# Issuing the middle result store from GpSimd instead of SyncE, in a row-wise ReLU-sum kernel

## The chip, the core and the metric

The kernel runs on one core of one Trainium2 chip. The metric is device time in microseconds for one execution of the whole program; for the kernel before, three runs were made and their median is given. A profile is one further execution, taken by the hardware profiler. It covers the span from the first to the last instruction that belongs to the kernel; the time of the execution is somewhat longer than the span.

## What is computed

```python
def setup_inputs():
    batch, seq, dim = 32, 512, 1024
    return {"x": np.random.randn(batch, seq, dim).astype(np.float32)}

def reference(x):
    relu_x = np.maximum(x, 0)
    return np.sum(relu_x, axis=-1).astype(np.float32)
```

There are 32 x 512 = 16384 rows of 1024 floats. Each row gives one float: the sum of its positive elements. 67.1 MB are read, 65.5 KB are written.

## The kernel before

**Layout.** The 16384 rows are spread over 128 partitions, so each partition handles J = 128 rows, called columns 0 to 127 here, as each ends up in one column of the result tile `res` (128 x 128 floats). The columns are cut into three regions, `REGIONS = [1, 111, 16]`. Within a region a partition's rows lie next to each other in memory, so a load of n columns is one contiguous run of n x 4 KB per partition, and a store of n columns is one run of n x 4 bytes per partition: 4 bytes for the first region, 444 for the middle one, 64 for the last.

**Loads.** All loads are issued by SyncE, in the order of the code, each with its own semaphore `s_in[...]` (a DMA raises its semaphore by 16 when it has landed). Seven chunks of 16 columns (`CHUNKS`; the first one in two DMAs, as it holds the one column of the first region and 15 of the middle one) go to three buffers in turn. From the fourth chunk on, SyncE first waits on `s_dve` until VectorE is done with that buffer. Then come tail loads of 8, 4 and 2 columns (line 103), and the last two columns in four pieces: three on line 114 (the last of these is counted by `s_in[-1]`) and one on line 117 that crosses from one row into the next, into the tile `seam`.

**Arithmetic.** For the first six chunks ScalarE applies ReLU in place to several columns at a time (line 147) and VectorE sums them (line 162), apart from some columns that either engine does alone. In the seventh chunk and the tail, and for the columns done alone, one instruction does both: `on_act` (line 129) on ScalarE, `on_dve` (line 132) on VectorE, each followed by a read of the accumulator. In the seventh chunk (lines 175 to 181) the two engines take alternate columns; the last column of each raises `s_fdve` and `s_fact`, and columns 1 to 111 of `res` are complete when both have passed. The pieces of the last two columns put partial sums into `seam`, and one closing instruction on each of ScalarE and VectorE (lines 205 and 207) adds them up and raises `s_last`.

**Stores.** There are three, all issued by SyncE behind the loads:

- Line 119, the first region: column 0 is transposed by VectorE into the tile `turned` (line 171), so that the 128 results leave as 4 runs of 128 bytes. It waits on `s_turn` and raises `s_store`.
- Line 125, the middle region: columns 1 to 111, 128 runs of 444 bytes, 55.5 KB. It waits on `s_fact`, `s_fdve` and `s_in[-1]`; the last of these is the landing of a load, not of a result that the store needs. It raises `s_store`, too.
- Line 211, the last region: columns 112 to 127, 128 runs of 64 bytes, 8 KB. It waits on `s_last` and raises `s_out`.

SyncE then waits until `s_store` has 32 and `s_out` has 16 (lines 212 and 213), and the program ends. SyncE's instructions run in order, so a wait holds up everything that is written behind it on SyncE. GpSimd has no work in the kernel; it only fills four constants at the start.

Of the kernel before, what the change touches and what calls it, by code (L numbers as in the profile page):

```python
# [7 lines left out]
REGIONS = [1, 111, 16]  # L8
# [10 lines left out]
def bass_relu_sum_kernel(  # L19
# [26 lines left out]
    start = [sum(REGIONS[:i]) for i in range(len(REGIONS))]  # L46
# [4 lines left out]
    ov = [of[P * s : P * (s + n)].rearrange("(p j) -> p j", p=P) for s, n in zip(start, REGIONS)]  # L51
# [4 lines left out]
    res = nc.alloc_sbuf_tensor("res", [P, J], fp32)  # L56
# [3 lines left out]
    s_in = [nc.alloc_semaphore(f"s_in{i}") for i in range(n_in)]  # L60
    s_act = nc.alloc_semaphore("s_act")
    s_dve = nc.alloc_semaphore("s_dve")
    s_fact = nc.alloc_semaphore("s_fact")
    s_fdve = nc.alloc_semaphore("s_fdve")
# [2 lines left out]
    s_last = nc.alloc_semaphore("s_last")  # L67
    s_turn = nc.alloc_semaphore("s_turn")
    s_store = nc.alloc_semaphore("s_store")
    s_out = nc.alloc_semaphore("s_out")  # L70

    sp, act, dve = nc.sync, nc.scalar, nc.vector

    NTWO = len(ACT_STEPS)
    done = [sum(map(len, DVE_STEPS[: c + 1])) for c in range(NTWO)]
# [11 lines left out]
    for c in range(NBIG + 1):  # L87
        if c >= NB:
            sp.wait_ge(s_dve, done[c - NB])
        if c < NBIG:  # L90
            i = 0
            for g, j, n in CHUNKS[c]:
                sp.dma_start(  # L93
                    out=buf[:, c % NB, i : i + n, :], in_=xv[g][:, j : j + n, :]
# [18 lines left out]
    for k, (lo, hi) in enumerate((first, second, third)):  # L113
# [5 lines left out]
    sp.dma_start(  # L119
        out=of[0:P].rearrange("(k q) -> k q", q=32), in_=turned[0:P:32, 0:32]  # L120
    ).then_inc(s_store, 16)
    sp.wait_ge(s_fact, 1)
    sp.wait_ge(s_fdve, 1)
    sp.wait_ge(s_in[-1], 16)
    sp.dma_start(out=ov[1][:, :], in_=res[:, start[1] : start[2]]).then_inc(s_store, 16)


    def on_act(t, acc):
# [11 lines left out]
    for c in range(NTWO):  # L140
# [17 lines left out]
        for n in DVE_STEPS[c]:  # L158
            if ready[r + n - 1] > seen:
# [3 lines left out]
                out=res[:, c * BIG + r : c * BIG + r + n],  # L163
                in_=buf[:, c % NB, r : r + n, :],
# [44 lines left out]

    sp.wait_ge(s_last, 2)  # L210
    sp.dma_start(out=ov[-1][:, :], in_=res[:, start[-1] : J]).then_inc(s_out, 16)
    sp.wait_ge(s_store, 16 * (len(REGIONS) - 1))
    sp.wait_ge(s_out, 16)


# [26 lines left out]
```

## Time and profile before

| What | Value |
|---|---|
| median of 3 runs | 160.79 us (160.7 to 160.81) |
| the profiled execution, its time | 160.84 us |
| its span | 159.5 us |
| VectorE busy | 120.7 us (76%), 59 instructions |
| ScalarE busy | 101.5 us (64%), 54 instructions |
| GpSimd busy | 0.2 us, 4 instructions |
| read from memory, mean | 67.11 MB, 421 GB/s over the span |
| granted clock | 1.00 |

The profile's engines are PE (TensorE, unused here), DVE (VectorE), ACT (ScalarE), POOL (GpSimd) and SP (SyncE). A name with a q at its end, such as SPq, is that engine's instruction queue: waits, and the issuing of DMAs, which do not count as busy. `L125` is line 125 of the kernel. In the timeline a row has its start in us, its length in us, engine, line, operation, and the tiles written and read. A view by windows gives, for each stretch of the span, the busy time of each engine, the granted clock, the mean busy share of the 16 DMA engines, and the GB/s that they moved. The time from a DMA's issue to its landing is printed for those whose landing some instruction waited for last.

### The profile page before, as it was taken

The page shows a single profiled execution, that of the slowest core. Times are in us where ns is not written, and L with a number is a line of the kernel's source. Part 1 is how long each engine was busy: PE and PEld are TensorE (multiplying, and loading weights), DVE is VectorE, ACT ScalarE, POOL GpSimd, SP SyncE. Part 2 cuts the span into 40 slices and gives each one's busy share as a digit, 9 for nine tenths or more (in the row PEclk, how much of TensorE's full clock was granted, in tenths as well). Part 3 has the DMA queues.
Part 4 walks back from the last instruction along what each step waited for, and adds up shares of the span by engine and source line. Part 5 has one row for each costly group of instructions (what it writes and reads, how often), then busy time and mean ns, then how long its engine had stood idle before and what let it go on. Part 6 is the DMA issues. An engine that isn't in the chain of part 4 may idle for free.

```text
span 159.5 us, 150 instructions
## 1 busy us (share of the span) xinstructions
DVE 120.7 (76%) x59; ACT 101.5 (64%) x54; POOL 0.2 (0%) x4
## 2 busy tenths in 40 slices
DVE  0000000009999999999999999999999999898995
ACT  3000059990799708996099951999329990496975
POOL 0000000000000000000000000000000000000000
DMA  9997996996996998989969969969969989798994
GB/s 378 493 401 339 493 526 263 526 526 263 526 510 279 526 427 362 526 362 427 526 263 526 526 263 526 526 263 526 493 296 526 427 362 526 312 469 378 419 403 142
DMA packets 2457, 67.18 MB, mean 421 GB/s; under 512 B 536, under 2 KB 792, under 8 KB 1176
## 3 DMA queue, kind: packets, MB, share of 16 engines
q1 hardware_dynamic: 2456, 67.18, 98.1%
q14 instruction: 1, 0.01, 0.0%
HBM read 67.11 MB, written 0.07 MB: 421 GB/s over the span
## 4 chain that ended last, share of the span: by engine, by line
DVE 54%; DMA 34%; ACT 9%; SPq 1%; issue 0%
DVE res L162 54%; DMA buf<-in_x_dram 34%; ACT buf L147 9%; SPq L103 1%; SPq L114 0%; DVE seam L132 0%; SPq L93 0%; ACT buf L129 0%; DVE turned L171 0%
## 5 line engine op out<-in xcount | busy, mean ns | idle before, releaser
L162 DVE TENSOR_REDUCE res<-buf 128x4 f32<-128x4096 f32 (+4 forms) x16 | 99.3, 6275 | 35.6 <-ACT buf L147 35.6
L147 ACT ACTIVATE buf<-buf 128x7168 f32<-128x7168 f32 (+5 forms) x13 | 80.4, 6233 | 46.2 <-DMA buf<-in_x_dram 46.2
L129 ACT ACTIVATE buf<-buf 128x1024 f32<-128x1024 f32 (+2 forms) x19 | 18.9, 994 | 9.0 <-DMA buf<-in_x_dram 8.9
L132 DVE TENSOR_SCALAR_CACHE_REDUCE buf<-buf 128x1024 f32<-128x1024 f32 (+3 forms) x20 | 20.9, 1099 | 1.7 <-DMA buf<-in_x_dram 1.5
L129 ACT ACTIVATION_READ_ACCUMULATOR buf<-buf 128x1 f32 x19 | 3.5, 186 | 0.0
L147 ACT ACT_TABLE_LOAD x1 | 1.3, 1283 | 1.3 <-PEq L227 1.3
L132 DVE DVE_READ_ACCUMULATOR buf<-buf 128x1 f32 x20 | 1.7, 83 | 0.0
L132 DVE TENSOR_SCALAR_CACHE_REDUCE seam<-seam 128x227 f32<-128x227 f32 x1 | 0.4, 391 | 0.0
L129 ACT ACTIVATE seam<-seam 128x114 f32<-128x114 f32 x1 | 0.3, 298 | 0.0
L171 DVE STREAM_TRANSPOSE turned<-res 128x32 f32<-128x32 f32 x1 | 0.2, 211 | 0.0
L129 ACT ACTIVATION_READ_ACCUMULATOR seam<-seam 128x1 f32 x1 | 0.2, 186 | 0.0
L227 POOL MEMSET const-bfloat16-1.0<- 128x1 bf16 x1 | 0.1, 102 | 0.0
L227 POOL MEMSET const-uint8-127<- 128x1 uint8 x1 | 0.1, 102 | 0.0
L227 POOL MEMSET const-float32-0.0<- 128x1 f32 x1 | 0.1, 99 | 0.2 <-issue 0.2
L227 POOL MEMSET const-float32-1.0<- 128x1 f32 x1 | 0.1, 99 | 0.0
L132 DVE DVE_READ_ACCUMULATOR seam<-seam 128x1 f32 x1 | 0.1, 81 | 0.0
## 6 DMA issues: line engine op xcount, KB each, us to landing
buf<-in_x_dram SPq DMA_DIRECT2D x1, 7680.0 KB, 21.2
buf<-in_x_dram SPq DMA_DIRECT2D x1, 4096.0 KB, 25.5
buf<-in_x_dram SPq DMA_DIRECT2D x1, 2048.0 KB, 30.1
buf<-in_x_dram SPq DMA_DIRECT2D x1, 1024.0 KB, 32.1
buf<-in_x_dram SPq DMA_DIRECT2D x1, 512.0 KB, 3.4
buf<-in_x_dram SPq DMA_DIRECT2D x1, 456.0 KB, 32.7
buf<-in_x_dram SPq DMA_DIRECT2D x1, 312.0 KB, 33.1
seam<-in_x_dram SPq DMA_DIRECT2D x1, 168.0 KB, 32.7
```

The lines of the kernel that those rows point to most:

```text
L103: sp.dma_start(out=buf[:, tb, r : r + n, :], in_=xv[-1][:, r : r + n, :]).then_inc(s_in[NBIG + i], 16)
L129: return act.activation(t, t, AF.Relu, accum_out=acc)
L132: return dve.tensor_scalar(out=t, in0=t, scalar1=0.0, scalar2=None, op0=ALU.max, op1=ALU.add, accum_out=acc)
L147: act.activation(t, t, AF.Relu).then_inc(s_act, 1)
L162: dve.tensor_reduce(out=res[:, c * BIG + r : c * BIG + r + n], in_=buf[:, c % NB, r : r + n, :], axis=X, op=ALU.add,).then_inc(s_dve, 1)
L171: dve.transpose(out=turned[:, :], in_=res[:, 0:32]).then_inc(s_turn, 1)
L227: nc = _bacc.Bacc("TRN2", target_bir_lowering=False, num_devices=1)
```

## The change

The middle store and its three waits go to GpSimd's queue. The store gets a semaphore of its own, `s_bulk`. The transposed store alone raises `s_store` now, so SyncE's closing waits are three: `s_store` at 16, `s_bulk` at 16, `s_out` at 16. Loads, the transposed store and the last store stay on SyncE. One line is added near the top, so the middle store's issue is on line 126 and the last store's on line 212 afterwards.

```diff
+    s_bulk = nc.alloc_semaphore("s_bulk")
     s_out = nc.alloc_semaphore("s_out")
 
-    sp, act, dve = nc.sync, nc.scalar, nc.vector
+    sp, act, dve, pool = nc.sync, nc.scalar, nc.vector, nc.gpsimd
...
-    sp.wait_ge(s_fact, 1)
-    sp.wait_ge(s_fdve, 1)
-    sp.wait_ge(s_in[-1], 16)
-    sp.dma_start(out=ov[1][:, :], in_=res[:, start[1] : start[2]]).then_inc(s_store, 16)
+    pool.wait_ge(s_fact, 1)
+    pool.wait_ge(s_fdve, 1)
+    pool.wait_ge(s_in[-1], 16)
+    pool.dma_start(out=ov[1][:, :], in_=res[:, start[1] : start[2]]).then_inc(s_bulk, 16)
...
     sp.wait_ge(s_last, 2)
     sp.dma_start(out=ov[-1][:, :], in_=res[:, start[-1] : J]).then_inc(s_out, 16)
-    sp.wait_ge(s_store, 16 * (len(REGIONS) - 1))
+    sp.wait_ge(s_store, 16)
+    sp.wait_ge(s_bulk, 16)
     sp.wait_ge(s_out, 16)
```

## The prediction

> **What bounds the kernel now.** I read the page's chain of work first. It is a chain of the reductions and then of the loads, and it goes through no store until the very end:
>
> ```profile
> ## 4 chain that ended last, share of the span: by engine, by line
> DVE 54%; DMA 34%; ACT 9%; SPq 1%; issue 0%
> ```
>
> The store that is moved is issued at 157.22 us of a span of 159.5 us, so only the last 2.3 us are in question. The view of SyncE's queue waits says what SyncE stood at in that time (columns: who waited, for what, us in total, times, longest):
>
> ```profile
> SPq L124 <- DMA buf<-in_x_dram: 31.2, 1, 31.2
> ...
> SPq L213 <- DMA out_dram<-res: 1.1, 1, 1.1
> SPq L211 <- DVE seam L132: 0.4, 1, 0.4
> ```
>
> The reader is to see three things. The middle store (line 125) waits 31.2 us for the last load, s_in[-1], and nothing else holds it. After it, SyncE waits another 0.4 us for VectorE before the last store (line 211): SyncE was not late, VectorE was. And the end is the last store's landing. The timeline, cut to the last 3 us, gives the moments (start, duration, engine, line):
>
> ```profile
> 157.22 0.35 SPq L125 DMA_DIRECT2D out_dram<-res  x1
> ...
> 157.58 0.39 DVE L132 TENSOR_SCALAR_CACHE_REDUCE seam<-seam 128x227 f32<-128x227 f32 x1
> 157.78 0.19 ACT L129 ACTIVATION_READ_ACCUMULATOR seam<-seam 128x1 f32 x1
> 157.90 0.08 DVE L132 DVE_READ_ACCUMULATOR seam<-seam 128x1 f32 x1
> 158.00 0.34 SPq L211 DMA_DIRECT2D out_dram<-res  x1
> ```
>
> SyncE has finished issuing the middle store at 157.22 + 0.35 = 157.57, and VectorE's last instruction ends at 157.98; the last store starts 0.02 later. So SyncE has 0.43 us to spare, and taking the middle store off its queue cannot bring the last store forward. Where the two transfers' packets run is seen when the same stretch is cut into seven windows (window, length, DVE, ACT and POOL busy, granted clock, DMA share, GB/s):
>
> ```profile
> 157.20:157.57 0.37, 0.34 (x4) 0.35 (x2) 0.00 (x0) 1.00 0.00 0
> 157.57:158.08 0.51, 0.40 (x2) 0.39 (x2) 0.00 (x0) 1.00 0.00 0
> 158.08:158.43 0.35, 0.00 (x0) 0.00 (x0) 0.00 (x0) 1.00 0.57 163
> 158.43:158.84 0.41, 0.00 (x0) 0.00 (x0) 0.00 (x0) 1.00 0.00 0
> 158.84:159.06 0.22, 0.00 (x0) 0.00 (x0) 0.00 (x0) 1.00 0.42 38
> 159.06:159.32 0.26, 0.00 (x0) 0.00 (x0) 0.00 (x0) 1.00 0.00 0
> ```
>
> The 55.5 KB of the middle store move from 158.08 to 158.43: 0.86 us after the issue began, for 0.35 us (163 GB/s x 0.35 us = 57 KB, so it is this store). The 8 KB of the last store move from 158.84 to 159.06, also 0.84 us after its issue. The wait at line 213 ends at 159.44 (158.00 + 0.34 + the 1.1 us waited), which is 0.38 us after the last packet; its instruction then closes the span at 159.47. The middle store's landing is not printed. With the same 0.38 us after its last packet it is there at 158.43 + 0.38 = 158.81, which is 1.59 us after its issue and **0.63 us before the end**. That slack decides this change.
>
> **The change, part by part.**
>
> Removed from SyncE: three waits and one DMA issue of 0.35 us, at a place where SyncE then stands idle for 0.4 us. Gain: 0. The loads and the transposed store stand ahead of it on SyncE's queue and were issued by 125.9 us; they don't move. Behind it stand only line 211 and the closing waits. SyncE will wait for s_last from 125.9 us on instead of for the last load; the release at 157.98 is VectorE's in either case, so line 211 stays at 158.00.
>
> Added to GpSimd: the same three waits. GpSimd's only work is four MEMSETs before 0.5 us, so nothing is queued behind these waits and the wait itself is free: s_fact and s_fdve fall by 147.1 us (the last rows of the seventh chunk end there), s_in[-1] by 157.2, as for SyncE today. Then one DMA issue with 128 rows of 444 bytes. **Its price is the unknown**, since no row of this trace shows a DMA issued by GpSimd. Of the 1.59 us from issue to landing, 0.73 (packets 0.35, landing 0.38) belong to the data and stay; the 0.86 us of preparation are what another issuer changes.
>
> Low bound: GpSimd prepares as fast as SyncE, or faster. At 0.86 us the store lands at 158.81; at the least, were the issue's own 0.35 us gone, at 158.46. Neither moves the end, because the last store then sets it: 0. Nothing earlier can be gained than that.
>
> High bound: the longest landing of a transfer that started on an idle queue is the first load, 512 KB in 3.4 us, nine times the bytes, with others beside it:
>
> ```profile
> buf<-in_x_dram SPq DMA_DIRECT2D x1, 512.0 KB, 3.4
> ...
> out_dram<-res SPq DMA_DIRECT2D x1, 8.0 KB, 1.4
> ```
>
> With 3.4 us the store lands at 157.22 + 3.40 = 160.62. I take the middle of 1.59 and 3.4, which is 2.50 us: bytes and packets are those of the low row, so the preparation alone can grow, and 2.50 us means 1.77 us for it, twice the 0.86 shown. I lean no nearer to the low row because every landing in this trace was prepared by SyncE, so no row speaks for GpSimd being as quick; and no nearer to the high row because nine times the bytes are in it. Landing then: 157.22 + 2.50 = 159.72. Its packets would run at about 158.99 to 159.34, beside the last store's (158.84 to 159.06); the most that these can take from it is their own busy time, 0.42 x 0.22 = 0.09 us. Landing 159.81.
>
> The closing waits: the one instruction of 28 ns at line 213 holds both semaphores today (the view of that line counts one); three semaphores ask for one more, 0.03 us each, all of them behind the landing where the middle store is last. End: 159.81 + 0.03 + 0.03 = 159.87.
>
> **Sum:** 159.87 - 159.47 = **+0.40 us**. The profiled execution took 160.84 us for its 159.47 us of span, so 1.37 us lie around it, taken as unchanged: 161.24. The median of the runs is 160.79, 0.05 below that execution, so **161.2 us** (+0.25%). A difference of 0.2%, 0.32 us, is about what a measurement of this kernel can tell from no change.
>
> A rule against the change: the Trainium skill, "DMA: Bandwidth & Descriptors", section "Issuing engines are not separate DMA queues", says that DMAs of all issuers share the same 16 engines and that spreading them saves only issue time; the windows agree in so far as 0.35 us of issue is all that SyncE loses to it here, and none of it counts. The same page's section "Latency and other measured facts" has the first byte at about 1 us for GpSimd's software path and 0.6 us for the hardware path, and "Anatomy of one DMA" fits 2.0 us + bytes/436e3 per DMA issued by GpSimd. By that fit the landing would be an estimated 157.22 + 2.13 = 159.35, just inside the slack, and the time unchanged. No run here shows it, and the sum above stands without it.
>
> **Rivals.**
>
> 1. *Hidden: no change.* GpSimd's landing takes under 2.2 us (it must be in by 159.44). For it: the slack of 0.63 us is real and three quarters of today's preparation. Against it: preparation has to stay under 0.86 + 0.63 = 1.49 us. Time: 160.79, or 160.82 with one more closing wait.
>
> 2. *Faster: the last store gains.* Place: line 211. Its issue at 158.00 falls while the middle store is still on the same path (packets until 158.43), and its own packets come at 158.84, 0.50 after its issue ended. If a part of this 0.50 were the middle store ahead of it, a queue of its own would give it back: at most all of it, so 160.3. It decides only while the middle store lands before the new end, that is by 158.95 (issue to landing 1.73). Against it: the middle store, on a queue that had issued nothing for 31 us, had the same gap (157.57 to 158.08, 0.51). An empty path gives no less, so the gain is nearer 0.
>
> 3. *First use.* GpSimd has done nothing for 157 us, and this is its only DMA; if a first use has to load something, as ScalarE does at its start (ACT_TABLE_LOAD, 1.28 us), that comes on top of the sum: 161.2 + 1.28 = 162.5. Nothing in the trace speaks for it on GpSimd.
>
> That the change fails to do what it says (SyncE still issues the store) is out: the issue is written on the other queue, and the trace will name it.
>
> **How the numbers follow.** The forecast, the middle store lands last at +0.05 to +1.3 us (the high bound: 160.62 + 0.09 + 0.06 = 160.77, or +1.30): 0.62. Hidden: 0.25. Faster by the last store: 0.06. First use: 0.07. Within the forecast's own 0.05 to 1.3 some four fifths lie above 0.32 us: slower 0.50 + 0.07 = 0.57; same 0.12 + 0.25 = 0.37; faster 0.06. The point is the likeliest case's, 161.2. The range takes in the hidden case and all but the last tenth of the forecast's: 160.7 to 162.0.
>
> **What would show it.** A POOL row of line 126 at 157.2 with nothing ahead of it; the last store still at 158.00; the 163 GB/s window no longer at 158.08 but behind 158.5; the closing waits ending on the middle store's semaphore instead of the last store's. If the packets of the two stores overlap, the last store's landing shifts by up to 0.1 us. I am wrong if packets of 444 bytes run before 158.7 (hidden), if line 211 issues at another time than 158.00, or if the stretch outside the span is not 1.37 us.

## The result, and the profile after

Over 15 runs each, taken together, the kernel after the change has a median of **161.11 us** (160.98 to 161.26) against 160.79 us (160.66 to 160.95) for the kernel before: a ratio of 1.0021, 95% interval [1.0014, 1.0028]. It is 0.32 us slower. The profiled execution took 161.10 us with a span of 159.8 us (159.75 by its last instruction), so 1.35 us lie around the span, against 1.37 before: the loss is inside it.

The timeline of the kernel after, cut to the last 2.7 us (start, length, engine, line, idle time before it and what ended that):

```profile
157.12 0.33 DVE L133 TENSOR_SCALAR_CACHE_REDUCE buf<-buf 128x176 f32<-128x176 f32 x1
...
157.49 0.39 DVE L133 TENSOR_SCALAR_CACHE_REDUCE seam<-seam 128x227 f32<-128x227 f32 x1
157.68 0.66 POOL L126 DMA_DIRECT2D out_dram<-res  x1 [157.24 <-DMA buf<-in_x_dram]
157.70 0.19 ACT L130 ACTIVATION_READ_ACCUMULATOR seam<-seam 128x1 f32 x1
157.81 0.08 DVE L133 DVE_READ_ACCUMULATOR seam<-seam 128x1 f32 x1
157.92 0.35 SPq L212 DMA_DIRECT2D out_dram<-res  x1
```

VectorE's last piece starts at 157.49, and at 157.58 before: in this execution the loads landed 0.09 us earlier, which has to be kept in mind when moments of the two are compared. The last store starts 0.03 us after VectorE's last instruction, so it gained nothing. The middle store's row on GpSimd starts at 157.68, although the load that it waits for has landed by 157.1 (VectorE starts on that piece at 157.12, the first row shown). Before the change VectorE started on the same piece at 157.20, and SyncE's row began only 0.02 us later, at 157.22:

```profile
157.20 0.33 DVE L132 TENSOR_SCALAR_CACHE_REDUCE buf<-buf 128x176 f32<-128x176 f32 x1
```

And GpSimd's row is 0.66 us long against SyncE's 0.35.

The DMA view has the issue to landing of both stores; before, it was 1.4 for the last one:

```profile
out_dram<-res POOLq DMA_DIRECT2D x1, 55.5 KB, 2.0
...
out_dram<-res SPq DMA_DIRECT2D x1, 8.0 KB, 1.4
```

SyncE's waits say which store ended last:

```profile
SPq L212 <- DVE seam L133: 32.1, 1, 32.1
...
SPq L214 <- DMA out_dram<-res: 1.4, 1, 1.4
```

Line 214 is the wait on `s_bulk`. It holds from 157.92 + 0.35 = 158.27 until about 159.67; line 215, `s_out`, waits for nothing any more, so the middle store now ends the program. Where the packets ran (window, length, DVE, ACT, POOL, clock, DMA share, GB/s):

```profile
157.68:158.34 0.66, 0.21 (x2) 0.20 (x2) 0.66 (x1) 1.00 0.00 0
158.34:158.76 0.42, 0.00 (x0) 0.00 (x0) 0.00 (x0) 1.00 0.00 0
158.76:158.92 0.16, 0.00 (x0) 0.00 (x0) 0.00 (x0) 1.00 0.52 48
158.92:159.26 0.34, 0.00 (x0) 0.00 (x0) 0.00 (x0) 1.00 0.56 169
159.26:159.75 0.49, 0.00 (x0) 0.00 (x0) 0.00 (x0) 1.00 0.00 0
```

The order of the two stores has turned round: the last store's 8 KB move from 158.76 and are all but over when the middle store's 55.5 KB begin at 158.92. From the start of its row to its packets GpSimd's store takes 1.24 us; SyncE's took 0.86. The packets themselves take as long as before (0.34 and 0.35 us).

### The profile page after: what moved, and what is told of

The parts are those of the page before. It is cut to its first block, busy times and chain, and to the rows that moved or that the text cites. A ratio compares the mean times of both kernels' runs of the same rounds, so it can differ in the third digit from the quotient of the medians.

```text
span 159.8 us, 151 instructions
## 1 busy us (share of the span) xinstructions
DVE 120.7 (76%) x59; ACT 101.5 (64%) x54; POOL 0.9 (1%) x5
## 4 chain that ended last, share of the span: by engine, by line
DVE 54%; DMA 34%; ACT 9%; SPq 2%; issue 1%; POOL 0%; POOLq 0%
DVE res L163 54%; DMA buf<-in_x_dram 34%; ACT buf L148 9%; SPq L104 1%; SPq L115 1%; POOL out_dram L126 0%; SPq L94 0%; DVE turned L172 0%; POOLq L125 0%
## 5 line engine op out<-in xcount | busy, mean ns | idle before, releaser
L126 POOL DMA_DIRECT2D out_dram<-res x1 | 0.7, 662 | 157.2 <-DMA buf<-in_x_dram 157.2
```

The source lines that it names most:

```text
L126: pool.dma_start(out=ov[1][:, :], in_=res[:, start[1] : start[2]]).then_inc(s_bulk, 16)
```

## The experiments

A store has landed when its semaphore has had all 16 increments. The trace's semaphore records, which the views above don't print, give these moments: the middle store's 16th increment came at 158.85 us before the change and at 159.65 after it, the last store's at 159.42 and 159.36. My theory after the result: GpSimd needs about 0.93 us more from release (the moment at which the last semaphore that the store waits for is there) to first packet, the slack of 0.57 us (159.42 - 158.85) hides a part of it, and the rest shows. The rivals: the closing waits, sharing of the DMA engines, any second queue, VectorE's work beside GpSimd, a first use.

**Earlier release, by 1.0 us and by 0.24 us.**

```diff
-    pool.wait_ge(s_in[-1], 16)
+    pool.wait_ge(s_in[-3], 16)      # e1_release3
+    pool.wait_ge(s_in[-2], 16)      # e2_release2
```

> GpSimd's middle store is released by the third-last load piece (s_in[-3]) instead of the last one, 1.0 us earlier; everything else as after the change. Theory (GpSimd needs about 0.93 us more than SyncE from release to first packet, and the end moves because the landing then passes the last store's): the store lands about 158.6 us, before the last store's 159.36, and the time returns to the kernel before, 160.79 (160.7 to 160.9). Rival (the loss is in SyncE's closing waits, in the sharing of the DMA engines or outside the span): it stays at 161.1.

> The same with s_in[-2], which lands 0.24 us before s_in[-1]. Theory: the landing comes 0.24 us earlier, 159.41 against 159.36 of the last store, so almost all of the loss goes: 160.85 to 160.92, between the two. If the loss is not a matter of lateness, 161.1.

e1_release3: 160.72 us against 160.77, ratio 0.9998 [0.9989, 1.0007]. The loss is gone with GpSimd still issuing the store, with three closing waits and a second queue, so none of these costs 0.3 us by itself, whatever the moment. What they cost when the two stores' packets meet this run doesn't tell, because here they lie 0.58 us apart.

e2_release2: 161.12 us (ratio 1.0026 [1.0015, 1.0037]), which is **not** what the theory said: released 0.24 us earlier, the kernel gained nothing. The DMA view of its profile shows where it went:

```profile
out_dram<-res POOLq DMA_DIRECT2D x1, 55.5 KB, 2.4
...
out_dram<-res SPq DMA_DIRECT2D x1, 8.0 KB, 2.1
```

Both stores land late, the last one by 0.7 us, though it is issued by SyncE as ever. That profile is of the slowest of seven runs (161.47 us), so the size is an extreme one; the median says that on most of them about half of it is there. The windows show the packets on top of each other:

```profile
158.20:158.78 0.58, 0.00 (x0) 0.00 (x0) 0.00 (x0) 1.00 0.00 0
158.78:158.96 0.18, 0.00 (x0) 0.00 (x0) 0.00 (x0) 1.00 1.07 316
158.96:159.14 0.18, 0.00 (x0) 0.00 (x0) 0.00 (x0) 1.00 0.44 41
159.14:159.21 0.07, 0.00 (x0) 0.00 (x0) 0.00 (x0) 1.00 0.19 14
159.21:160.10 0.89, 0.00 (x0) 0.00 (x0) 0.00 (x0) 1.00 0.03 9
```

The middle store moves from 158.78, the last store joins it at 158.97, and after the last packet 0.89 us pass without data of either store until the landing; before the change that was 0.37 us.

**The other way round: the last store on GpSimd.**

```diff
-    sp.wait_ge(s_last, 2)
-    sp.dma_start(out=ov[-1][:, :], in_=res[:, start[-1] : J]).then_inc(s_out, 16)
+    pool.wait_ge(s_last, 2)
+    pool.dma_start(out=ov[-1][:, :], in_=res[:, start[-1] : J]).then_inc(s_out, 16)
```

> The other way round: SyncE issues the middle store as before the change, GpSimd the last store, which has no slack and is released when VectorE has stopped. Theory (0.93 us more of preparation, of which the slack hid 0.57 in the change): the whole 0.93 shows, 161.7 (161.55 to 161.85). Rival (GpSimd's preparation was long only because VectorE was at work beside it): clearly under 161.5. Rival (the price goes by bytes per row, 64 here against 444): less than 161.7 as well, and packets earlier.

161.38 us, ratio 1.0035 [1.0022, 1.0049]: +0.61 us, below what the theory asked and above what the rivals did. The timeline says why:

```profile
158.33 0.66 POOL L211 DMA_DIRECT2D out_dram<-res  x1 [157.89 <-DVE seam L132]
```

The row starts 0.30 us after VectorE's end (158.03), where the change had some 0.6 us from landing to row. From row to packets it is 1.23 us (packets from 159.56), against 0.84 on SyncE. The row is 0.66 us long as in the change, with 64 bytes per row in place of 444 and with VectorE idle. So GpSimd's price has two parts: the row with what follows, about **0.39 us** more than SyncE both with 444 bytes per row beside a busy VectorE and with 64 beside an idle one, and the time from release to row, 0.30 here against 0.03 on SyncE. 0.30 - 0.03 + 0.39 = 0.66; measured are 0.61. The 0.93 us taken as one constant was wrong.

**The order of the closing waits.**

```diff
     sp.wait_ge(s_store, 16)
-    sp.wait_ge(s_bulk, 16)
     sp.wait_ge(s_out, 16)
+    sp.wait_ge(s_bulk, 16)
```

> After the change, with s_bulk waited for last of the three closing semaphores. Theory: from the landing to the end it is 0.108 us after the change against 0.045 before; with s_bulk last 0.04 to 0.06 us of that goes: 161.05. Rival (closing waits cost more than they show): 160.9 or less.

161.02 us, ratio to the kernel before 1.0014 [1.0005, 1.0023]; the change itself had 1.0021. By the semaphore records the span ends 0.045 us after the landing instead of 0.108, so the order of the closing waits is worth 0.06 us; by the medians it is 0.09, but these were taken on different occasions and are no sharper than that.

**Who carries the last wait.** In the change the waits on `s_in[-1]` and `s_fdve` became an instruction of their own ahead of the store, and the store carried the wait on `s_fact`, done long before. The order of the three lines decides that. SyncE's store before the change was split in the same way (line 124 is that instruction), and its row still began 0.09 us after the landing.

```diff
+    pool.wait_ge(s_in[-1], 16)      # e5_own_wait;  s_in[-2] in e6_own_wait2
     pool.wait_ge(s_fact, 1)
     pool.wait_ge(s_fdve, 1)
-    pool.wait_ge(s_in[-1], 16)
```

> After the change, with GpSimd's three waits in another order, so that the one that falls last (s_in[-1]) is carried by the store itself and no longer by a wait instruction ahead of it. The run with the last store on GpSimd had 0.30 us from release to the row's start with its own wait, the change 0.62 with the wait ahead. Theory 1 (that wait instruction costs about 0.3 us): the row starts at 157.34 instead of 157.68, packets 158.58 to 158.91. Theory 2 on top (packets of the two stores at the same time lengthen both landings, as with s_in[-2]): time 161.0 to 161.2 in spite of it. If lateness alone counts: 160.79 to 160.85.

> The same order of waits with s_in[-2] in place of s_in[-1]: released 0.24 us earlier again. Packets about 158.34 to 158.67, over before the last store's begin at 158.76. Theory 2 (only overlap lengthens the landings): 160.72 to 160.82. Rival (any GpSimd store this near to the last one lengthens it): 161.0 or more.

GpSimd's row in e5_own_wait:

```profile
157.48 0.66 POOL L126 DMA_DIRECT2D out_dram<-res  x1 [157.05 <-DMA buf<-in_x_dram]
```

It starts 0.29 us after the load's landing (157.48 against 157.20, by the semaphore record) instead of 0.64: on GpSimd the separate wait costs 0.35 us. Still the time is 161.06 us (ratio 1.002 [1.0011, 1.0028]). Its packets now run from 158.73, under the last store's:

```profile
158.15:158.73 0.58, 0.00 (x0) 0.00 (x0) 0.00 (x0) 1.00 0.00 0
158.73:158.91 0.18, 0.00 (x0) 0.00 (x0) 0.00 (x0) 1.00 1.07 316
158.91:159.09 0.18, 0.00 (x0) 0.00 (x0) 0.00 (x0) 1.00 0.46 42
159.09:159.15 0.06, 0.00 (x0) 0.00 (x0) 0.00 (x0) 1.00 0.17 12
159.15:159.70 0.55, 0.00 (x0) 0.00 (x0) 0.00 (x0) 1.00 0.00 0
```

The last store lands 0.55 us after its last packet instead of 0.37, and it is again the one that ends the program: the middle store is in at 159.51, the last one at 159.69. e6_own_wait2 puts the packets ahead of the last store's (158.51 to 158.84, then from 158.94): 160.86 us, ratio 1.0006 [0.9997, 1.0014], and the last store lands in 1.4 us again. The median is above the expected 160.82, but the interval takes in no change; its single runs go from 160.71 to 161.07.

**ScalarE's queue instead of GpSimd's.** The store is written behind ScalarE's closing instruction.

```diff
     on_act(seam[:, 0:k], res[:, J - 2 : J - 1]).then_inc(s_last, 1)
+    act.wait_ge(s_fact, 1)
+    act.wait_ge(s_fdve, 1)
+    act.dma_start(out=ov[1][:, :], in_=res[:, start[1] : start[2]]).then_inc(s_bulk, 16)
```

> ScalarE issues the middle store, behind its closing instruction: a queue of its own as in the change, but not GpSimd's. Theory (the loss is GpSimd's longer way from release to packets, not the leaving of SyncE's queue): issue near 157.6, first packet 0.85 later, landing near 159.2, time 160.75 to 160.9. Rival (any second queue beside the last store loses): 161.05 or more.

161.14 us, ratio 1.0027 [1.0018, 1.0035]. Issue (157.53), first packet (158.42) and landing (159.20) are where they were expected; the time is not. Its DMA view:

```profile
out_dram<-res ACTq DMA_DIRECT2D x1, 55.5 KB, 1.7
...
out_dram<-res SPq DMA_DIRECT2D x1, 8.0 KB, 1.7
```

The middle store's last packets (to 158.77) touch the last store's first (158.75), and the last store takes 1.7 us instead of 1.4. So the stretching is not GpSimd's alone. Not all of this run's loss is stretching: over its 11 runs 1.53 us lie around the span on average, against 1.36 for the kernel before, so some 0.17 of the 0.39 us lie outside it; what that is stayed open.

**A second DMA on GpSimd.** GpSimd issues the transposed store as well, from 70 us on.

```diff
-    sp.wait_ge(s_turn, 1)
-    sp.dma_start(
+    pool.wait_ge(s_turn, 1)
+    pool.dma_start(
         out=of[0:P].rearrange("(k q) -> k q", q=32), in_=turned[0:P:32, 0:32]
     ).then_inc(s_store, 16)
```

> GpSimd issues the transposed store as well, from 70.3 us on, so that the middle store is its second DMA. Theory (no first-use cost): the middle store's row is 0.66 us long and its packets begin 1.24 us after the row's start as in the change; time 161.05 to 161.15. Rival (part of it is a first use): a shorter row, time 160.9 or less.

161.30 us, ratio 1.0033 [1.0022, 1.0045]. GpSimd's own rows:

```profile
70.54 0.69 POOL L120 DMA_DIRECT2D out_dram<-turned  x1 [70.10 <-DVE turned L172]
157.62 0.56 POOL L126 DMA_DIRECT2D out_dram<-res  x1 [86.38 <-DMA buf<-in_x_dram]
```

The second row is 0.56 us long, and its packets begin 1.14 us after it started (1.24 for the first DMA of a program): by this profile GpSimd's first DMA costs about 0.1 us more than its second, but the time didn't fall as the rival had expected. For the quicker store collided: packets from 158.76, under the last store's, and that one took 2.0 us to land. Quicker on GpSimd, slower in all.

**No wait for the loads, on either queue.**

```diff
-    pool.wait_ge(s_in[-1], 16)      # e9_nowait, from the kernel after
-    sp.wait_ge(s_in[-1], 16)        # e11_sync_nowait, from the kernel before
```

> After the change without the wait on s_in[-1]: GpSimd's store goes when the seventh chunk's results are there, at 147.1 us, while the loads still run. Theory (lateness and overlap at the end are the whole loss): both are gone, and 57 KB among the loads cost up to 0.13 us at their 440 GB/s: 160.75 to 160.95. Rival (GpSimd's way holds up the loads): 161.1 or more.

> The kernel before without the wait on s_in[-1]: SyncE's middle store is issued at 147.1 us behind the loads already queued, its packets come right behind the last load's, about 157.1, and land near 157.6. Theory (in the kernel before the middle store is hidden): no change, 160.7 to 160.85. If its being near the last store costs anything before the change: 160.65 or less.

e11_sync_nowait: 160.81 us against 160.78, ratio 1.0 [0.9991, 1.0009]. The store is hidden before the change, and being near the last store costs nothing there. e9_nowait: 161.00 us, ratio 1.0014 [1.0005, 1.0023], between the two expectations. On a queue of its own GpSimd's store goes in among the loads (its packets run from 151.4 to 152.1) and the load of the tail's 4 columns (`s_in[8]`) landed at 152.93 instead of 152.44 before the change, by the semaphore records. Its single runs scatter from 160.83 to 161.41; how much of that is this one piece stayed open.

**Two close stores, both on SyncE.** The middle store waits for `s_last` and goes right ahead of the last one.

```diff
     sp.wait_ge(s_last, 2)
+    sp.wait_ge(s_fact, 1)
+    sp.wait_ge(s_fdve, 1)
+    sp.dma_start(out=ov[1][:, :], in_=res[:, start[1] : start[2]]).then_inc(s_store, 16)
     sp.dma_start(out=ov[-1][:, :], in_=res[:, start[-1] : J]).then_inc(s_out, 16)
```

> No GpSimd: SyncE issues the middle store only when s_last is there, right ahead of the last store, so that the two stores' packets follow each other without the 0.4 us of the kernel before. The last store is issued 0.35 us later for it. If stretched landings need two queues at once: 161.1 (160.77 + 0.35). If packets that follow closely are enough, whatever the queue: 161.3 or more.

162.18 us, ratio 1.0084 [1.007, 1.0098]: +1.40 us, far more than the later issue explains. SyncE's two rows, and the windows:

```profile
157.94 0.35 SPq L209 DMA_DIRECT2D out_dram<-res  x1
158.34 0.43 SPq L210 DMA_DIRECT2D out_dram<-res  x1
```

```profile
158.79:159.14 0.35, 0.00 (x0) 0.00 (x0) 0.00 (x0) 1.00 0.57 163
159.14:159.26 0.12, 0.00 (x0) 0.00 (x0) 0.00 (x0) 1.00 0.00 0
159.26:159.47 0.21, 0.00 (x0) 0.00 (x0) 0.00 (x0) 1.00 0.57 76
159.47:159.86 0.39, 0.00 (x0) 0.00 (x0) 0.00 (x0) 1.00 0.02 1
159.86:160.76 0.90, 0.00 (x0) 0.00 (x0) 0.00 (x0) 1.00 0.00 0
```

The parts add up: the last store's row starts 0.43 us after VectorE's end instead of 0.03 (0.40 more), its first packet comes 0.92 us after that instead of 0.84 (0.08), its packets last 0.59 us instead of 0.21 (0.38), and the landing follows 0.90 us after them instead of 0.37 (0.53): 1.39 together. The two stores' packets are 0.13 us apart. But the 0.38 seems to have a cause of its own. By the packet records 8 of the last store's 128 data packets, one sixteenth, straggle until 159.85; the others are over at 159.47. The stragglers begin at 159.79, just when a packet of 8 KB on the instruction queue (159.26 to 159.79) is over; in every other run of the table such a packet begins only after the last store's data. That it held them up is what the times suggest, not what a run shows. The 15th of the 16 increments came at 160.04, 0.57 us after the other packets (the landing before the change: 0.37), and the 16th at 160.75. If the 16th is that of the straggling share, a stretch of some 0.2 us is left that owes nothing to the instruction packet; more than that this run can't show for two stores on SyncE alone.

Together, by the packet and semaphore records of one profile each (us; "to landing" is from the store's last data packet to its 16th increment):

| Run | middle store's packets | to landing | last store's packets | to landing | median |
|---|---|---|---|---|---|
| before | 158.08-158.41 | 0.44 | 158.84-159.05 | 0.37 | 160.79 |
| e1_release3 | 157.83-158.15 | 0.39 | 158.73-158.94 | 0.37 | 160.72 |
| e6_own_wait2 | 158.51-158.83 | 0.44 | 158.94-159.15 | 0.37 | 160.86 |
| e7_act | 158.42-158.77 | 0.44 | 158.75-158.95 | 0.61 | 161.14 |
| e8_warm | 158.76-159.12 | 0.59 | 158.94-159.18 | 0.72 | 161.30 |
| e2_release2 | 158.78-159.13 | 0.79 | 158.97-159.20 | 0.90 | 161.12 |
| e5_own_wait | 158.73-159.08 | 0.43 | 158.92-159.14 | 0.55 | 161.06 |
| after | 158.92-159.25 | 0.40 | 158.76-158.97 | 0.39 | 161.11 |
| e10_sync_late | 158.80-159.13 | 0.42 | 159.26-159.85 | 0.90 | 162.18 |

So there are three cases. With the middle store early enough (before, e1_release3, e6_own_wait2) the last store ends the program and lands as ever. With the middle store late (after) the last store's packets go first and land as ever, and the middle store ends the program. In between, when the last store's packets fall on the middle store's or right behind them, the last store ends the program, but its landing stretches by 0.2 to 0.5 us (in e10_sync_late with the instruction packet in it). The gap from which it is safe isn't settled: 0.11 us was clean in e6_own_wait2, 0.13 was not in e10_sync_late. No version beat the kernel before; e1_release3 equals it.

## Why the prediction was right

**Right: what decides, and the sign.** The middle store lands last, the last store stays where it was, SyncE's 0.35 us were worth nothing, and the loss is what GpSimd's way exceeds the slack by. e1_release3 shows it from the other side. The slack itself was 0.57 us and not 0.63: the middle store lands 0.44 us after its packets, where the 0.38 of the last store had been taken.

**Right by luck of its parts: the preparation.** The middle of two far bounds put the first packet at 158.99; it came at 158.92 in an execution 0.09 us ahead, so 159.01 on the old clock. But 1.77 us of preparation are not one thing twice as slow. Measured against SyncE: the row starts 0.55 us later after the same landing (0.64 against 0.09), 0.35 of which go when the store itself carries the last wait; from row to packets it is 0.38 more (1.24 against 0.86). No run had shown either part, and the bounds know nothing of the order of the waits: for e5_own_wait they would have given the same 2.50 us, and its store landed 0.30 us sooner after its release (2.31 us against 2.61).

**Mis-sized: the overlap.** "The most that these can take from it is their own busy time", 0.09 us. In the change itself the last store took near 0 from the middle one (packets 0.33 us as before, landing 0.40 us behind them against 0.44). As a bound it fails where the packets meet: in e2_release2 the middle store landed 0.79 us after its packets, 0.35 more than before, and the last one 0.90, 0.53 more, where the prediction had at most 0.1. It did no harm here, as GpSimd was late enough for the last store to go first.

**Small, but under-sized: the closing waits.** From the landing to the span's end 0.06 us were predicted; by the records it is 0.108, against 0.045 before.

**The sum** was +0.40. On the old clock the span after ends at 159.84, which is +0.38 (before, it ended at 159.468): the overlap took 0.09 less than predicted, and the closing waits (0.05) and the first packet (0.02) took more. The medians say +0.32; the last 0.06 lie between one profiled execution and the median of 15.

**The rivals.** "Hidden" was given the condition that the store be in by 159.44. e5_own_wait was quicker by 0.35 us and lost as much as the change: to be a little quicker was no way to be hidden, because then the last store's landing stretched. The gain at the last store didn't come (1.4 us to landing in both). A first use costs 0.1 us (e8_warm) and not 1.28.

The Trainium skill's page "DMA: Bandwidth & Descriptors", section "Latency and other measured facts", has the first byte 0.4 us later on GpSimd's path; the runs agree for what follows the row's start (0.39), and show 0.3 to 0.6 us from release to row on top. The fit in its section "Anatomy of one DMA", 2.0 us + bytes/436e3, gave an estimated 2.13 us; measured are 1.97 from the row's start but 2.61 from the load's landing, and the latter is what a schedule feels. The same page's section "Queues, rings and completion order" says that a semaphore's increment lands only after every earlier write of the same DMA engine, across its queues. The stretched landings fit that rule, ScalarE's, GpSimd's and SyncE's alike; no run here takes the ordering itself away, so it stays an explanation that fits and isn't shown.

## What to carry to other kernels

Before moving a store to another queue, find the landing that ends the program and the slack of the moved one against it: here the queue was idle 0.43 us and the slack was 0.57, so there was nothing to gain, and 0.3 us were lost. On GpSimd reckon from the release, not from the row: here it took 0.3 us to the row when the store carried the wait that falls last, 0.6 when that wait stood ahead of it, then 1.24 us to the first packet. Keep other stores' packets clear of the last store's. When what a store waits for isn't what it needs, an earlier release can do that: 1.0 us earlier the whole loss was gone (e1_release3), 0.24 us earlier none of it (e2_release2).

## What was not expected of the hardware

- A small store whose packets come on top of another store's, or close behind them, lands late, beside GpSimd's, ScalarE's and SyncE's store alike: from issue to landing 2.0 us (e8_warm), 1.7 (e7_act) and 2.4 (e10_sync_late, with an instruction packet in the way) against 1.4.
- In e10_sync_late a packet of 8 KB on the instruction queue took 0.53 us, and one sixteenth of the last store's data began only when it was over, 0.32 us after the rest had ended.
- The order in which three waits are written moved a GpSimd store by 0.35 us (row 0.64 and 0.29 us after the landing); SyncE's row, with the same order as the slower of the two, had begun 0.09 us after it.
- GpSimd's store left in 16 packets of 3552 bytes where SyncE's left in 128 of 444 bytes, and both took 0.33 us.
- The second DMA of a program on GpSimd had a row of 0.56 us, the first 0.66 to 0.69.
